# Joining the lower halves of seven-product pairs, two kinds of split buffers, three temporaries

## The chip, the cores and the metric

The kernel runs on one core of a Trainium2 chip. The metric is the device time of one execution in microseconds, as the median over several runs. Beside it there is one profiled execution, from which all rows of views are taken.

## The reference, cut to what matters

```python
D_MODEL, SEQ, D_FF = 2048, 256, 8192            # batch 1, 2 layers

def sq_relu_mlp(h, w1, w2):
    return jnp.square(jax.nn.relu(h @ w1)) @ w2

def reference(x, ...):
    for layer in range(2):
        h = rms_norm(x, norm_mixer_g[layer])
        if layer == 0:
            x = x + conv_module(h, ...)          # 2048x4096, depthwise 31, layer norm, 2048x2048
        else:
            x = x + mla(h, ...)                  # latent attention, 16 heads
        h = rms_norm(x, norm_mlp_g[layer])
        x = x + sq_relu_mlp(h, mlp_w1[layer], mlp_w2[layer])
    return rms_norm(x, final_norm_g)
```

Everything is float32. There are four stages: convolution, MLP 0, attention, MLP 1. The two MLPs multiply 256 rows by a 2048x8192 and an 8192x2048 matrix each.

## The kernel before

**Split products.** TensorE (PE) works on a rounded format (`F32R`), so each float32 operand is held as an upper part (the rounded copy) and a lower part (what the rounding left). A product is three matmuls: upper with upper, lower with upper, upper with lower (`mm3`, L201 to L205). The activations' parts are the stationary operand and the weights' parts are the moving one, 512 columns at a time; in the first product of an MLP it is the other way round (L655, L656).

**Streaming the weights.** `load` (L153) brings a tile `raw` of 128 x 2048 float32 from memory by a DMA that SyncE issues; there are three such buffers. A tile is split in two halves of 1024 columns: ScalarE copies the upper part (`hi`, L170), then VectorE subtracts it from the raw values and writes the lower part (`lo`, L174). `hi` and `lo` each go through one ring of `WB` = 6 buffers of 128 x 1024 (4 KB in each partition) that lives in `wpool` and is used by every stage. In the convolution and the attention the order of this work is written out by hand; in the MLPs a planner of the tile framework orders each engine's instructions from the program's order and from when operands are ready. On the chip every engine runs its own list in that order.

**An MLP** treats the 8192 inner columns in two halves (`hf`). For each half there is an up phase and a down phase.

The up phase has 8 groups `g` of 4 units; a unit is one raw tile and 32 pairs of matmuls into four accumulators. After a group, L673 to L677 add the two parts of the sums, square the positive values and scale them with a row `r2_row`. Then the result is split, plainly (L686, L687) or by `mixed_inputs`.

The down phase makes two sweeps over the 2048 output columns, each over one pair of 512-column blocks (class `Sums`, eight accumulators, all banks of PSUM). Its inner 32 blocks of 128 rows are taken two at a time, 16 pairs in a sweep. Eight of these (seven in the last half of MLP 1; the table `MIXED`) are **seven-product pairs**: the 2x2 block product of rows t, columns c and inner blocks j is made with seven products in place of eight by the Strassen-Winograd scheme, that is 21 matmuls instead of 24. The other pairs are plain. For a seven-product pair the weights need seven pieces of 512 columns: three blocks as they are (b11, b21, b22) and four sums (t1 to t4). `mixed_weights` (L490 to L510) makes them from one raw tile: a split of b11 and b21 (1024 columns), a split of b22 (512), three subtractions in place in the raw tile (L505 with 1024 columns, L506 and L507 with 512), a split of t1 and t3, a split of t4 and t2. That is four upper and four lower parts and three subtractions. `mixed_inputs` (L512 to L529) does the like for the activations, once for each pair in the up phase.

**Ending a sweep.** The four accumulators `u` of the seven-product pairs take part in several outputs. When the last of these pairs is done, `join` (L582 to L593) copies the first sum u1 to a temporary on ScalarE, forms three more sums on VectorE in three more temporaries, and adds the four results to the residual `xs` by `put`: by an accumulating DMA that GpSimd (POOL) issues where `by_dma` is set (five of the eight sweeps), else by VectorE. `close` (L595 to L605) adds the four other accumulators, in those sweeps two of them through temporaries copied by ScalarE and the DMA. The temporaries are the tiles `v` of the up phase, four buffers.

The very last sweep goes through `product_A`, which holds the splits of its last three units, finishes the rows of t = 0 first and then those of t = 1 in two halves of columns, so that the final norm can begin early.

The functions that the change touches, with the line numbers of the profile:

Of the kernel before, what the change touches and what calls it, by code (L numbers as in the profile page):

```python
# [18 lines left out]
P = 128  # L19
D = 2048  # L20
KC = D // P
T = 2
# [57 lines left out]
def trunk_kernel(  # L80
# [31 lines left out]
    wpool = ctx.enter_context(tc.tile_pool(name="wpool", bufs=2))  # L112
    small = ctx.enter_context(tc.tile_pool(name="small", bufs=2))
    psum, psum_cx = {}, [ExitStack()]

    def repool(name, **banks):

# [22 lines left out]
    def nm(s):  # L140
        uid[0] += 1
        return f"{s}_{uid[0]}"
# [21 lines left out]
    def upper_half(raw, h):  # L164

        _, nj, cols = raw.shape
        js = slice(h * nj // 2, (h + 1) * nj // 2)
        hi = wpool.tile([P, nj // 2, cols], F32R, tag="hi", name=nm("hi"), bufs=WB)
        lo = wpool.tile([P, nj // 2, cols], F32R, tag="lo", name=nm("lo"), bufs=WB)
        nc.scalar.activation(hi, raw[:, js, :], AF.Copy)  # L170
        return hi, lo, raw[:, js, :]

# [317 lines left out]
    def mixed_weights(raw):  # L490

        def halves(src):
            hi = wpool.tile(list(src.shape), F32R, tag="hi", name=nm("hi"), bufs=WB)
            lo = wpool.tile(list(src.shape), F32R, tag="lo", name=nm("lo"), bufs=WB)
            nc.scalar.activation(hi, src, AF.Copy)  # L497
            nc.vector.tensor_tensor(lo, src, hi.bitcast(F32), op=ALU.subtract)  # L498
            return [(hi[:, i, :], lo[:, i, :]) for i in range(src.shape[1])]
# [5 lines left out]
        nc.vector.tensor_tensor(top, raw[:, :, NB:], top, op=ALU.subtract)  # L505
        nc.vector.tensor_tensor(low[:, 1, :], low[:, 1, :], top[:, 0, :], op=ALU.subtract)  # L506
        nc.vector.tensor_tensor(low[:, 0, :], low[:, 0, :], low[:, 1, :], op=ALU.subtract)  # L507
        t1, t3 = halves(top)
        t4, t2 = halves(low)
        return b11, b21, b22, t1, t2, t3, t4  # L510

    def mixed_inputs(v, fh, fl):  # L512

        def halves(src, at, n):
            hi, lo = fh[:, at : at + n, :], fl[:, at : at + n, :]
            nc.scalar.activation(hi, src, AF.Copy)
            nc.vector.tensor_tensor(lo, src, hi.bitcast(F32), op=ALU.subtract)

        a = v.rearrange("p k (t n) -> p (k t) n", t=T)
# [4 lines left out]
        nc.vector.tensor_tensor(a21, a11, a21, op=ALU.subtract)  # L526
        nc.vector.tensor_tensor(a11, a22, a11, op=ALU.subtract)
        nc.vector.tensor_tensor(a12, a12, a11, op=ALU.subtract)
        halves(a, 3, 4)  # L529

    class Sums:
# [14 lines left out]
        def mixed(self, w, k, fh, fl, end):  # L546

            b11, b21, b22, t1, t2, t3, t4 = mixed_weights(load([rows(w, k, 2, self.n * NB, 2 * NB)], 2))
            u1, u6, u7, u5 = self.u
            work = [  # L550
                (u1, 0, b11), (u5, 6, t1), (u7, 4, t3), (u6, 3, t2),
                (self.e[0][0], 1, b21), (self.e[0][1], 5, b22), (self.e[1][0], 2, t4),
            ]
# [28 lines left out]
        def join(self, room):  # L582

            u1, u6, u7, u5 = self.u
            a, b, c, d = (room() for _ in range(4))
            nc.scalar.activation(a, u1, AF.Copy)
            self.put(0, 0, a if self.by_dma else u1)
            nc.vector.tensor_tensor(b, u6, a, op=ALU.add)
            nc.vector.tensor_tensor(c, u7, b, op=ALU.add)
            nc.vector.tensor_tensor(d, u5, c, op=ALU.add)  # L590
# [18 lines left out]
    def mlp(layer, ssq, next_gain, finish=None, before=None, beside=None, after_up=None):  # L609

        with ExitStack() as cx:
            mp = cx.enter_context(tc.tile_pool(name=f"mp{layer}", bufs=1, reuse_waits="tile"))
            nkh = FF // P // HALVES
            ng = nkh // 4
            nssq = None
            r2_row = mp.tile([P, S], F32, name=nm("r2_row"))
            repool(f"mlp{layer}", acc=8)

            def v_tile():
                return mp.tile([P, 2, S], F32, tag="v", name=nm("v"), bufs=4)  # L620

            def room():
                return v_tile().rearrange("p a n -> p (a n)")
# [10 lines left out]
            for hf in range(HALVES):  # L634
# [4 lines left out]
                gs = {}  # L639
                for g in range(ng):  # L640
                    ps = [acc_tile() for _ in range(4)]
                    if layer > 0 and hf == g == 0:
# [20 lines left out]
                    if g in mixed or g in plain[len(plain) + len(mixed) - N_MIXED :]:  # L663
                        shape = [P, 2, 7, P] if g in mixed else [P, 4, S]
                        gs[g] = [mp.tile(shape, F32R, tag=f"s{c}", name=nm(f"s{c}"), bufs=N_MIXED) for c in "hl"]
                    else:
                        gs[g] = [mp.tile([P, 4, S], F32R, tag=f"g{c}", name=nm(f"g{c}"), bufs=ng - N_MIXED) for c in "hl"]
                    gh, gl = gs[g]
                    for b2 in range(2):
                        v = v_tile()  # L670
                        for b in range(2):
                            o = ps[2 * b2 + b]
                            nc.scalar.activation(v[:, b, :], o[:, S:], AF.Copy)  # L673
                            nc.vector.tensor_tensor(v[:, b, :], o[:, :S], v[:, b, :], op=ALU.add)
                        nc.vector.scalar_tensor_tensor(out=v, in0=v, scalar=0.0, in1=v, op0=ALU.max, op1=ALU.mult)
                        row = r2_row.rearrange("p (a n) -> p a n", a=1).broadcast_to([P, 2, S])
                        nc.vector.tensor_tensor(v, v, row, op=ALU.mult)  # L677
                        if 2 * g + b2 in ms:
                            mixed_inputs(v, gh[:, b2], gl[:, b2])
                            continue  # L680
                        if g in mixed:
                            v = v.rearrange("p k (t n) -> p (k t) n", t=T)
                            h, l = gh[:, b2, : 2 * T, :], gl[:, b2, : 2 * T, :]
                        else:
                            h, l = (a[:, 2 * b2 : 2 * b2 + 2, :] for a in (gh, gl))
# [4 lines left out]

                def at_kt(i):
                    def at(k, t):
                        a = gs[k // 4][i]
                        if k // 4 in mixed:
                            return a[:, k % 4 // 2, k % 2 * T + t, :]
                        return a[:, k % 4, t * P : (t + 1) * P]
                    return at

                hi, lo = at_kt(0), at_kt(1)
# [1 line left out]
                due, rest = [], []  # L701

                def mixed_quad(sums, i):
                    g, b = divmod(ms[i], 2)
                    sums.mixed(w, k_lo + 4 * g + 2 * b, gs[g][0][:, b], gs[g][1][:, b], i == len(ms) - 1)

                split_end = last and finish is not None
                for n in range(0, NNB - 2 * split_end, 2):
# [599 lines left out]

    def rotary_tables(pool):

        place = pool.tile([P, 2, S], F32, tag="v", name=nm("v"), bufs=4).rearrange("p a n -> p (a n)")
        at = [0]

        def room(n):
# [629 lines left out]
```

## Time and profile before

| | |
|---|---|
| median of 3 runs | 1934.01 us (1933.93 to 1934.53) |
| profiled execution | 1934.31 us, its span 1932.5 us |
| TensorE matmuls (PE) | 1921.0 us busy, 10725 instructions |
| TensorE weight loads (PEld) | 1681.5 us |
| VectorE (DVE) | 1592.2 us, 2457 instructions |
| ScalarE (ACT) | 1095.6 us, 1636 instructions |
| GpSimd (POOL) | 249.0 us |
| DMA | 375.5 MB, mean 194 GB/s |

The profile is of one execution. Its span reaches from the first to the last instruction; the 1.8 us between the span and the execution's time lie around it. Busy times of the engines overlap. PE and PEld are the same engine's matmuls and loads of the stationary operand. A group or timeline row names the line of the kernel, the engine, the operation, what it writes and reads, the shapes and a count; "idle before" and the arrow tell how long the engine stood still and what it waited for. Line numbers can be a helper's: L170 and L174 are all plain splits, L203 to L205 all `mm3` products, L497 and L498 the splits of seven-product pairs.

### The profile page before, as it was taken

Reading aid. Unit: us, or ns where it says so; the run is one execution under the profiler, and the core shown is the slowest. Engines: PE = TensorE matmul, PEld = TensorE weight load, DVE = VectorE, ACT = ScalarE, POOL = GpSimd, SP = SyncE. Lnnn points to the kernel's source line nnn. Section 1 sums busy time; section 2 is a strip of 40 time slices with the busy share of each in tenths; the row PEclk is TensorE's granted clock in tenths of the full one; section 3 lists DMA queues with packets and bytes.
Section 4 is the critical chain, followed back from the end, with each engine's and each line's share of the span. In section 5 each row is a group of like instructions: output and inputs, shape, how many; then the busy total and the mean of one; then the engine's idle time right before and its main releaser. Section 6 shows DMA issues by size and latency. Waiting matters only on the chain.

```text
span 1932.5 us, 28477 instructions
## 1 busy us (share of the span) xinstructions
PE 1921.0 (99%) x10725; PEld 1681.5 (87%) x10725; DVE 1592.2 (82%) x2457; ACT 1095.6 (57%) x1636; POOL 249.0 (13%) x208
## 2 busy tenths in 40 slices
PE   9999999999999999999999999999999999999998
PEld 8999888888888888888898998888888888888887
DVE  7999988877999776799976766877789987678998
ACT  5667755554555545555576655555555554455554
POOL 6999200000010100000001420000000010000000
PEclk9999999999999999999999999999999999999999
DMA  7766456665585866655656545465646776665774
GB/s 230 214 183 189 153 189 206 193 194 177 175 251 194 263 195 187 194 174 196 217 176 175 142 134 192 155 216 186 188 162 225 222 248 212 191 196 175 231 219 150
DMA packets 230427, 375.50 MB, mean 194 GB/s; under 512 B 16392, under 2 KB 107792, under 8 KB 230032
## 3 DMA queue, kind: packets, MB, share of 16 engines
q1 hardware_dynamic: 224640, 363.28, 58.7%
q0 software_dynamic: 4320, 7.87, 2.2%
q10 hardware_dynamic: 1328, 2.52, 0.4%
q8 instruction: 84, 1.38, 0.3%
q14 instruction: 55, 0.45, 0.1%
HBM read 363.68 MB, written 2.10 MB: 189 GB/s over the span
## 4 chain that ended last, share of the span: by engine, by line
PE 97%; DVE 2%; DMA 0%; ACT 0%; issue 0%; ACTq 0%; DVEq 0%
PE acc L655 24%; PE acc L205 15%; PE acc L203 15%; PE acc L204 15%; PE acc L656 13%; PE acc L823 8%; PE acc L1287 2%; DVE sum L910 1%; DMA xs<-in_x 0%; PE acc L1535 0%; PE acc L1566 0%; PE acc L1565 0%; PE acc L1536 0%; PE acc L1564 0%; PE acc L1537 0%; PE tr L267 0%
## 5 line engine op out<-in xcount | busy, mean ns | idle before, releaser
L174 DVE TENSOR_TENSOR lo<-raw,hi 128x1024 fp32r<-128x1024 f32 (+2 forms) x509 | 602.2, 1197 | 232.3 <-ACT hi L170 226.6
L170 ACT ACTIVATE hi<-raw 128x1024 fp32r<-128x1024 f32 (+2 forms) x574 | 583.9, 1036 | 361.1 <-PE acc L655 203.7
L655 PE MATMUL acc<-xt,hi 128*128 128x512 f32 x2048 | 710.6, 390 | 0.0
L656 PE MATMUL acc<-xt,lo 128*128 128x256 f32 x2048 | 577.5, 282 | 0.0
L655 PEld LDWEIGHTS acc<-xt,hi 128*128 128x128 f32 x2048 | 384.3, 188 | 80.7
L656 PEld LDWEIGHTS acc<-xt,lo 128*128 128x128 f32 x2048 | 387.1, 189 | 0.2
L497 ACT ACTIVATE hi<-raw 128x1024 fp32r<-128x1024 f32 x248 | 228.7, 948 | 228.3 <-DVE raw L505 134.0
L498 DVE TENSOR_TENSOR lo<-raw,hi 128x1024 fp32r<-128x1024 f32 x248 | 263.9, 1087 | 27.6 <-ACT hi L497 22.5
L203 PE MATMUL acc<-hi,sh 128*128 128x512 f32 x514 | 200.1, 389 | 0.0
L205 PE MATMUL acc<-lo,sh 128*128 128x512 f32 x514 | 200.1, 389 | 0.0
L203 PE MATMUL acc<-hi,gh 128*128 128x512 f32 (+1 forms) x516 | 200.0, 388 | 0.0
L205 PE MATMUL acc<-lo,gh 128*128 128x512 f32 (+1 forms) x516 | 199.9, 387 | 0.0
L204 PE MATMUL acc<-hi,gl 128*128 128x512 f32 (+1 forms) x516 | 199.9, 387 | 0.0
L823 PE MATMUL acc<-xt,hi 128*128 128x256 f32 x1024 | 180.2, 281 | 0.3 <-ACT b L1106 0.2
L204 PE MATMUL acc<-hi,sl 128*128 128x512 f32 x450 | 175.1, 389 | 0.0
L578 POOL DMA_DIRECT2D xs<-v x30 | 26.5, 994 | 1136.4 <-DVE lo L174 703.2
L910 DVE SCALAR_TENSOR_TENSOR sum<-ub,w_dw,sum 128x256 f32<-128x256 f32 x409 | 164.3, 481 | 3.6 <-ACT sum L880 3.0
L174 POOL TENSOR_TENSOR lo<-raw,hi 128x1024 fp32r<-128x1024 f32 x65 | 155.0, 2410 | 17.3 <-ACT hi L170 17.3
L823 PEld LDWEIGHTS acc<-xt,hi 128*128 128x128 f32 x1024 | 154.8, 188 | 1.1 <-ACT xt L1090 0.6
L823 PE MATMUL acc<-xt,lo 128*128 128x256 f32 x512 | 139.2, 279 | 0.0
L205 PEld LDWEIGHTS acc<-lo,sh 128*128 128x128 f32 x514 | 96.5, 188 | 20.4 <-DVE lo L498 0.3
L204 PEld LDWEIGHTS acc<-hi,gl 128*128 128x128 f32 x516 | 96.9, 188 | 19.9
(314 smaller groups left out, 2531.3 us busy)
## 6 DMA issues: line engine op xcount, KB each, us to landing
raw<-in_mlp_w SPq DMA_DIRECT2D x255, 1024.0 KB, 5.5
raw<-in_conv_w_pw SPq DMA_DIRECT2D x62, 512.0 KB, 5.1
raw<-in_conv_w_pw SPq DMA_DIRECT2D x16, 1024.0 KB, 5.1
raw<-in_mla_w_o SPq DMA_DIRECT2D x16, 1024.0 KB, 5.7
raw<-in_mla_w_kv_up SPq DMA_DIRECT2D x32, 256.0 KB, 3.9
xs<-v POOLq DMA_DIRECT2D x30, 256.0 KB, 7.8
raw<-in_mla_w_in SPq DMA_DIRECT2D x8, 576.0 KB, 3.8
raw<-in_mla_w_in SPq DMA_DIRECT2D x4, 1024.0 KB
```

Of the source, the lines that this page charges most:

```text
L170: nc.scalar.activation(hi, raw[:, js, :], AF.Copy)
L174: eng.tensor_tensor(lo, raw, hi.bitcast(F32), op=ALU.subtract)
L203: nc.tensor.matmul(ps, sh, mh, start=start, stop=False)
L204: nc.tensor.matmul(ps, sl, mh, start=False, stop=False)
L205: nc.tensor.matmul(ps, sh, ml, start=False, stop=stop)
L497: nc.scalar.activation(hi, src, AF.Copy)
L498: nc.vector.tensor_tensor(lo, src, hi.bitcast(F32), op=ALU.subtract)
L655: nc.tensor.matmul(ps[b], wh[:, bs], xhl(k), start=k == 0, stop=False)
L656: nc.tensor.matmul(ps[b][:, :S], wl[:, bs], xh(k), start=False, stop=k == KC - 1)
L823: nc.tensor.matmul(pss[c][b][:, :S], w[i][:, bs], (xh, xl)[j](k), start=k == i + j == 0, stop=end and k == k0 + nk - 1 and (i, j) == terms ...
L910: nc.vector.scalar_tensor_tensor(out=out, in0=ubs[c][:, w : w + S], scalar=tap(c, w), in1=base, op0=ALU.mult, op1=ALU.add)
L1287: nc.tensor.matmul(ps2[b][t], x_kt(k, t), w[:, bs], start=k == g == i == 0, stop=k == KC - 1 and i == len(group) - 1,)
```

## The change

- **Joined halves.** `mixed_weights` looks at the raw tile as four pieces and splits three of them, b21, b22 and b11, as one tile of 1536 columns. The first subtraction takes 1024 columns with one operand that repeats one piece and another that reads two pieces backwards. Two subtractions of 512 columns and two splits of 1024 follow. `mixed_inputs` splits three of the four untouched pieces at once. The numbers of the products in `Sums.mixed` follow the new places.
- **Two kinds of split buffers.** The buffers are no longer one ring in `wpool`: each stage opens a pool of its own (`open_halves`), at the same place in memory. The convolution and the attention have six and six as before. In the MLPs there are two of kind "a" (for the first half of a plain tile and for the 1536 columns, 6 KB in each partition) and three of kind "b" (for the second half and for the 1024-column splits of a seven-product pair), of upper and lower parts each.
- **Three temporaries.** `join` uses one temporary again, and the `v` tiles have three buffers. u1 is always added to the residual by VectorE.
- The tiles for the split activations are arranged by pairs instead of groups, and `r2_row` lies in an existing scratch tile. `MIXED` is the same.

```diff
-N_MIXED = 4
+SPLIT_BUFS = {"a": 2, "b": 3}
...
+    def open_halves(cx, name, kinds=False):
+        halves_of[:] = [cx.enter_context(tc.tile_pool(name=name, bufs=1, reuse_waits="tile"))]
+        two_kinds[0] = kinds
+
+    def in_halves(shape, kind=None):
+        kind = kind if two_kinds[0] else None
+        n = WB if kind is None else SPLIT_BUFS[kind]
+        return [halves_of[0].tile(shape, F32R, tag=c + (kind or ""), name=nm(c), bufs=n) for c in ("hi", "lo")]
...
-        hi = wpool.tile([P, nj // 2, cols], F32R, tag="hi", name=nm("hi"), bufs=WB)
-        lo = wpool.tile([P, nj // 2, cols], F32R, tag="lo", name=nm("lo"), bufs=WB)
+        hi, lo = in_halves([P, nj // 2, cols], "ab"[h])
         nc.scalar.activation(hi, raw[:, js, :], AF.Copy)
...
-        b11, b21 = halves(raw[:, :, :NB])
-        (b22,) = halves(raw[:, 1:2, NB:])
-        top = raw[:, 0, :].rearrange("p (c n) -> p c n", c=2)
-        low = raw[:, 1, :].rearrange("p (c n) -> p c n", c=2)
-        nc.vector.tensor_tensor(top, raw[:, :, NB:], top, op=ALU.subtract)
-        nc.vector.tensor_tensor(low[:, 1, :], low[:, 1, :], top[:, 0, :], op=ALU.subtract)
-        nc.vector.tensor_tensor(low[:, 0, :], low[:, 0, :], low[:, 1, :], op=ALU.subtract)
-        t1, t3 = halves(top)
-        t4, t2 = halves(low)
+        r = raw.rearrange("p j (c n) -> p (j c) n", c=2)
+        h1, l1 = in_halves([P, 3, NB], "a")
+        nc.scalar.activation(h1, r[:, :3, :], AF.Copy)
+        nc.vector.tensor_tensor(l1, r[:, :3, :], h1.bitcast(F32), op=ALU.subtract)
+        nc.vector.tensor_tensor(
+            r[:, 2:4, :], r[:, 3:4, :].broadcast_to([P, 2, NB]), r[:, 2:0:-1, :], op=ALU.subtract
+        )
+        nc.vector.tensor_tensor(r[:, 1, :], r[:, 1, :], r[:, 2, :], op=ALU.subtract)
+        nc.vector.tensor_tensor(r[:, 0, :], r[:, 0, :], r[:, 1, :], op=ALU.subtract)
+        b21, b22, b11 = ((h1[:, i, :], l1[:, i, :]) for i in range(3))
+        t = []
+        for i in (2, 0):
+            h2, l2 = in_halves([P, 2, NB], "b")
+            nc.scalar.activation(h2, r[:, i : i + 2, :], AF.Copy)
+            nc.vector.tensor_tensor(l2, r[:, i : i + 2, :], h2.bitcast(F32), op=ALU.subtract)
+            t += [(h2[:, j, :], l2[:, j, :]) for j in range(2)]
+        t1, t3, t4, t2 = t
...
-        a11, a21, a12, a22 = (a[:, i, :] for i in range(4))
-        halves(a[:, 0:1, :], 0, 1)
-        halves(a[:, 2:4, :], 1, 2)
+        a12, a22, a11, a21 = (a[:, i, :] for i in range(4))
+        halves(a[:, 0:3, :], 0, 3)
...
-            a, b, c, d = (room() for _ in range(4))
+            a, c, d = (room() for _ in range(3))
             nc.scalar.activation(a, u1, AF.Copy)
-            self.put(0, 0, a if self.by_dma else u1)
-            nc.vector.tensor_tensor(b, u6, a, op=ALU.add)
-            nc.vector.tensor_tensor(c, u7, b, op=ALU.add)
+            x = self.place(0, 0)
+            nc.vector.tensor_tensor(x, u1, x, op=ALU.add)
+            nc.vector.tensor_tensor(a, u6, a, op=ALU.add)
+            nc.vector.tensor_tensor(c, u7, a, op=ALU.add)
             nc.vector.tensor_tensor(d, u5, c, op=ALU.add)
-            nc.vector.tensor_tensor(b, u5, b, op=ALU.add)
-            for (t, n), o in (((1, 0), c), ((1, 1), d), ((0, 1), b)):
+            nc.vector.tensor_tensor(a, u5, a, op=ALU.add)
+            for (t, n), o in (((1, 0), c), ((1, 1), d), ((0, 1), a)):
                 self.put(t, n, o)
...
+            open_halves(cx, f"halves{layer}", kinds=True)
...
-            r2_row = mp.tile([P, S], F32, name=nm("r2_row"))
+            r2_row = scratch[:, :S]
...
-                return mp.tile([P, 2, S], F32, tag="v", name=nm("v"), bufs=4)
+                return mp.tile([P, 2, S], F32, tag="v", name=nm("v"), bufs=3)
...
+        open_halves(cx, "halvesc")
...
+        open_halves(cx, "halvesa")
```

More of the change, by code (lines that the diff above doesn't have):

```diff
@@ L550, in mixed @@
             work = [
-                (u1, 0, b11), (u5, 6, t1), (u7, 4, t3), (u6, 3, t2),
-                (self.e[0][0], 1, b21), (self.e[0][1], 5, b22), (self.e[1][0], 2, t4),
+                (u1, 2, b11), (u5, 4, t1), (u7, 6, t3), (u6, 5, t2),
+                (self.e[0][0], 0, b21), (self.e[0][1], 3, b22), (self.e[1][0], 1, t4),
             ]
@@ L662, in mlp @@
                         beside = None
-                    if g in mixed or g in plain[len(plain) + len(mixed) - N_MIXED :]:
-                        shape = [P, 2, 7, P] if g in mixed else [P, 4, S]
-                        gs[g] = [mp.tile(shape, F32R, tag=f"s{c}", name=nm(f"s{c}"), bufs=N_MIXED) for c in "hl"]
-                    else:
-                        gs[g] = [mp.tile([P, 4, S], F32R, tag=f"g{c}", name=nm(f"g{c}"), bufs=ng - N_MIXED) for c in "hl"]
-                    gh, gl = gs[g]
+                    both = [2 * g, 2 * g + 1]
+                    if g % 2 == 0:
+                        tiles = [mp.tile([P, 2, 7, P], F32R, tag=f"s{c}", name=nm(f"s{c}"), bufs=ng // 2) for c in "hl"]
+                        for b2, p in enumerate(both):
+                            fs[p] = [a[:, b2] for a in tiles]
+                    elif g == 1:
+                        fs[2] = [mp.tile([P, 7, P], F32R, tag=f"o{c}", name=nm(f"o{c}")) for c in "hl"]
+                        fs[3] = [mp.tile([P, 2 * T, P], F32R, tag=f"p{c}", name=nm(f"p{c}")) for c in "hl"]
+                    else:
+                        tiles = [mp.tile([P, 2, 2 * T, P], F32R, tag=f"g{c}", name=nm(f"g{c}"), bufs=ng // 2 - 1) for c in "hl"]
+                        for b2, p in enumerate(both):
+                            fs[p] = [a[:, b2] for a in tiles]
                     for b2 in range(2):
@@ L703, in mixed_quad @@
                 def mixed_quad(sums, i):
[L704 to L705 removed]
+                    sums.mixed(w, k_lo + 2 * ms[i], *fs[ms[i]], i == len(ms) - 1)
                 split_end = last and finish is not None
@@ L1309, in rotary_tables @@
     def rotary_tables(pool):
-        place = pool.tile([P, 2, S], F32, tag="v", name=nm("v"), bufs=4).rearrange("p a n -> p (a n)")
+        place = pool.tile([P, 2, S], F32, tag="v", name=nm("v"), bufs=3).rearrange("p a n -> p (a n)")
         at = [0]
```

26 lines of the change are left out of this document (8 added, 18 removed).

## The prediction, on record before the change was run

> **What bounds the kernel now.** I read the page first: busy time by engine, then the chain that ended last.
>
> ```profile
> span 1932.5 us, 28477 instructions
> ...
> PE 1921.0 (99%) x10725; PEld 1681.5 (87%) x10725; DVE 1592.2 (82%) x2457; ACT 1095.6 (57%) x1636; POOL 249.0 (13%) x208
> ...
> PE 97%; DVE 2%; DMA 0%; ACT 0%; issue 0%; ACTq 0%; DVEq 0%
> ```
>
> TensorE is busy for 99% of the span and carries 97% of the chain. VectorE at 82% and ScalarE at 57% are behind it. Then the windows by stage (columns: length, then busy us and count of PE, PEld, DVE, ACT, POOL, then clock and DMA).
>
> ```profile
> 300.00:478.00 178.00, 178.00 (x1029) 157.75 (x1028) 139.41 (x242) 95.47 (x140) 0.00 (x0) 1.00 0.60 190
> 478.00:560.00 82.00, 82.00 (x364) 67.91 (x363) 77.30 (x86) 45.79 (x53) 3.65 (x4) 1.00 0.60 196
> 641.00:819.00 178.00, 178.00 (x1027) 157.73 (x1027) 126.15 (x187) 90.77 (x128) 1.77 (x2) 1.00 0.66 205
> 1842.00:1924.50 82.50, 82.50 (x377) 68.78 (x375) 76.58 (x97) 46.55 (x65) 1.75 (x2) 1.00 0.58 183
> 1924.50:1932.50 8.00, 0.23 (x2) 0.03 (x1) 3.18 (x12) 1.42 (x3) 0.00 (x0) 0.77 0.37 131
> ```
>
> In the MLPs PE has no gap: an up phase (the first product, 1024 matmuls) takes 178.0 us and a sweep of the down phase (the second product, one pair of 512-column blocks) about 82. Two up phases agree at 178.0 although VectorE is busy for 139 us in one and 126 us in the other: its load does not set their pace. VectorE fills 94% of a sweep, so there it is close behind. The change leaves PE's matmuls as they are, so it can win only where PE waits now, and that is little. It can lose wherever it makes a split arrive late.
>
> **What is saved.** These are the groups, shapes apart (count, then busy us, mean ns).
>
> ```profile
> L498 DVE TENSOR_TENSOR lo<-raw,hi 128x1024 fp32r<-128x1024 f32 x186 | 225.5, 1221 | 27.6 <-ACT hi L497 22.5 <-PE acc L205 0.6
> L497 ACT ACTIVATE hi<-raw 128x1024 fp32r<-128x1024 f32 x186 | 195.0, 1058 | 222.3 <-DVE raw L505 134.0 <-DVE raw L507 34.5 <-PE acc L204 23.6
> L505 DVE TENSOR_TENSOR raw<-raw 128x1024 f32<-128x1024 f32 x62 | 75.5, 1218 | 0.2
> L507 DVE TENSOR_TENSOR raw<-raw 128x512 f32<-128x512 f32 x62 | 42.8, 691 | 1.7
> L498 DVE TENSOR_TENSOR lo<-raw,hi 128x512 fp32r<-128x512 f32 x62 | 42.4, 684 | 0.0
> L497 ACT ACTIVATE hi<-raw 128x512 fp32r<-128x512 f32 x62 | 38.4, 619 | 6.0 <-PE acc L204 5.9
> ```
>
> A seven-product pair now costs VectorE four 1024-column and three 512-column operations, ScalarE three and one. Joined, one 1024 and one 512 become one 1536. Columns beyond 512 cost 1221 − 684 = 537 ns per 512, so a 1536 takes about 1.76 us. Against 1.22 + 0.68 that saves 0.15 us of latency per pair. Operations overlap, though: in the timeline below two 1024 splits span 2.35 us, so they start 1.13 to 1.14 us apart, less than the 1.22 that one lasts. By start to start the saving is about 0.07 us. Over 62 pairs it is 4 us (by latency 9) of VectorE time, and about as much of ScalarE's; 31 pairs of inputs lose one small operation on each engine too. All of it lies beside PE, so it is worth 0.
>
> The Trainium skill ("Perfetto Trace Analysis", section "Optimizing Scalar/DVE Operations") gives about 60 ns of overhead per VectorE instruction, half of what is seen as latency: by it the saving is an estimate of 62 × 0.06 = 3.7 us, and the trace's 0.07 and 0.15 agree. The same section says that where these engines are not saturated but cause bubbles on others, "breaking up instructions may allow work to be completed sooner", which speaks against joining here; that is the late first product weighed next.
>
> **The joined tile comes whole.** Its first product (b11) waits for 1536 columns instead of 1024: 0.54 us later on ScalarE, and later again on VectorE. This matters where two seven-product pairs follow each other.
>
> ```profile
> 838.97 1.82 DVE L498 TENSOR_TENSOR lo<-raw,hi 128x1024 fp32r<-128x1024 f32 x2
> 840.71 1.22 DVE L505 TENSOR_TENSOR raw<-raw 128x1024 f32<-128x1024 f32 x1
> 836.70 2.35 DVE L174 TENSOR_TENSOR lo<-raw,hi 128x1024 fp32r<-128x1024 f32 x2
> 847.47 1.22 DVE L505 TENSOR_TENSOR raw<-raw 128x1024 f32<-128x1024 f32 x1
> 850.06 2.52 DVE L498 TENSOR_TENSOR lo<-raw,hi 128x1024 fp32r<-128x1024 f32 x2
> 851.43 0.39 PE L203 MATMUL acc<-hi,sh 128*128 128x512 f32 x1
> ```
>
> Pair after pair VectorE needs 847.47 − 840.71 = 6.76 us; a plain pair needs 838.97 − 836.70 = 2.27. PE starts a matmul every 0.2267 us (1841.91 to 1842.14 in a row below is one), so a seven-product pair gives it 21 × 0.2267 = 4.76 us of work and a plain one 24 × 0.2267 = 5.44. VectorE loses 2.0 us of lead per seven-product pair and gains 3.2 per plain one. Here the lower part of the fifth product's weights is ready at 850.06 + 1.2 = 851.3, 0.15 us ahead of its first matmul. It is wanted only in the third matmul, 0.45 later, so 0.6 us is left. The wait of a joined copy (0.4 us) eats most of that. For the three sweeps that begin with two such pairs I take 0.1 each, 0.3 together (0 to 3).
>
> **The rings.** Before, one ring of six hi and six lo buffers runs through the whole program, and a split goes ahead six half units. Now it is two "a" and three "b" in the MLP, laid out anew in the same memory at each stage. Inside an up phase "a" and "b" alternate every half unit of 178.0 / 64 = 2.78 us. With two "a" tiles a unit's first half can be filled only once the first half of the unit two before it is used up: 2 × 5.56 − 2.78 − (1.06 + 1.22 + a little for the two hand-overs) leaves a lead of some 5.9 us. That is enough and costs 0.
>
> **Borders of the stages.** Old and new tiles of a border share memory. Before, only the next free slot of the ring counted. I laid the tiles out by size and order: hi at 0 to 24 KB and lo at 24 to 48 KB with six each; in the MLP a-hi, a-lo, b-hi, b-lo at 0, 12, 24 and 36 KB. From convolution to MLP the first "a" tile falls on one free in time: 0. From MLP 0 to attention the first lower part falls on the last "b" tile, which PE reads until the MLP ends at 984.04.
>
> ```profile
> 976.11 0.75 DVE L174 TENSOR_TENSOR lo<-raw,hi 128x576 fp32r<-128x576 f32 x1
> 984.66 1.27 DVE L601 TENSOR_TENSOR xs<-acc,xs 128x512 f32<-128x512 f32 x2
> 984.04 0.29 PE L203 MATMUL acc<-hi,xt 128*128 128x288 f32 x1
> ```
>
> That split now ends at 976.9; then it can start only at about 984.4, lasts 0.75, and is wanted 0.3 us after 984.04: a stall of 0.9 us if VectorE takes it first, 2.1 if it adds the two sums first (L601). Queued behind it are the next splits and the last sums. I take 1.5 (0 to 2.6). From attention to MLP 1 the first "a" lower tile falls on the attention's last split.
>
> ```profile
> 1239.67 1.23 DVE L174 TENSOR_TENSOR lo<-raw,hi 128x1024 fp32r<-128x1024 f32 x1 [1.49 <-ACT hi L170]
> 1240.84 1.37 DVE L388 TENSOR_TENSOR xs<-acc,xs 128x512 f32<-128x512 f32 x2
> 1241.32 0.40 PE L655 MATMUL acc<-xt,hi 128*128 128x512 f32 x1
> ```
>
> The split that is now begun at 1239.67 waits until 1241.3 + 0.4 and, behind the two sums, begins at about 1242.2 and ends at 1243.4; it is wanted by the second matmul at 1241.55: 1.9 us (0 to 2.4).
>
> **The last sweep**, from 1842, has the least lead of all. Before, its first seven-product pair is copied early, into the free ring.
>
> ```profile
> 1836.14 1.58 ACT L497 ACTIVATE hi<-raw 128x1024 fp32r<-128x1024 f32 x2 [3.16 <-DMA raw<-in_mlp_w]
> 1842.48 0.59 ACT L604 ACTIVATE v<-acc 128x512 f32<-128x512 f32 x1
> ...
> 1841.91 0.39 PE L205 MATMUL acc<-lo,gh 128*128 128x512 f32 x1
> 1842.14 0.39 PE L203 MATMUL acc<-hi,gh 128*128 128x512 f32 x1
> ...
> 1890.73 2.52 DVE L498 TENSOR_TENSOR lo<-raw,hi 128x1024 fp32r<-128x1024 f32 x2
> 1891.78 0.39 PE L203 MATMUL acc<-hi,sh 128*128 128x512 f32 x1
> ```
>
> With two "a" tiles, both still read by the sweep before until about 1841.5, that copy moves from 1836.14 to 1841.5, and with it VectorE's seven operations, 1 to 4 us later than now since it can do other splits meanwhile. At 1891.78 no lead is left today (the lower part ends at 1890.73 + 1.2 = 1891.9, wanted at 1892.2), and a plain pair with a seven-product pair gives back only 3.2 − 2.0 = 1.2 us each time. I take a stall of 2.5 us in sum, from 0 (lead regained by then) to 5.
>
> **Three temporaries, sums, tail.**
>
> ```profile
> xs<-v POOLq DMA_DIRECT2D x30, 256.0 KB, 7.8
> 1836.03 0.86 POOL L578 DMA_DIRECT2D xs<-v  x1 [6.68 <-DVE v L589]
> 1839.47 1.78 POOL L578 DMA_DIRECT2D xs<-v  x2 [2.58 <-DVE v L590]
> ```
>
> Five sweeps add by DMA; of their 30 DMAs five become VectorE additions (5 × 0.69 = 3.4 us, beside PE). But the first temporary, whose DMA was issued early, is now free only after the last of three: two left at 1839.47, and ScalarE's copy into a temporary at 1842.48 would wait until a landing up to 7.8 us after issue, with the next upper parts queued behind it. First products into those banks come a plain pair (5.4 us) later, so I take 0.5 for all (0 to 5). In the tail the last block holds three units' splits until the end, with two "a" tiles for them: 0.4 (0 to 3), on top of the 8 us of 1924.50 to 1932.50.
>
> **Sum:** 0 + 0.3 + 0 + 1.5 + 1.9 + 2.5 + 0.5 + 0.4 = 7.1 us on the profiled execution of 1934.31, which is 0.3 above the median of 1934.01. On the median: 1941.1.
>
> **The rivals.**
> 1. *Nothing is late.* The tiles do not collide as I laid them out, or other work is put in front, and the lead carries the last sweep: 1934 to 1937.5, say 1935.5. For it: PE's only visible wait inside the MLPs now is nearly nil, and leads of 6 us remain. Against: the last sweep's lead of zero.
> 2. *The joined subtraction with one half repeated and one read backwards runs at half pace.* A pair would need 6.76 + 1.2 us and a pair with a plain one 10.2, all that PE has (4.76 + 5.44): no lead is regained, each of seven sweeps would lose about 2 to 3 us more, 1955. No row has a reversed operand; one that is repeated is read at the normal pace:
>
> ```profile
> 391.68 0.69 DVE L677 TENSOR_TENSOR v<-v,r_row 128x512 f32<-128x512 f32 x1
> ```
>
> 3. *The tail or the temporaries decide:* ScalarE blocked 5 us in each of two sweeps, or the last block put in another order: 1948 to 1955.
> 4. *Faster:* the up phases' pace is set by a waiting hi/lo split. 512 pairs at 0.2267 + 0.1133 would take 174.1 us instead of 178.0; all four at that pace would give 1934.0 − 15.6 = 1918.4. It decides from about 1 us per phase on. Against: the same 178.0 us at unequal loads.
>
> **How the numbers follow.** This kernel can be told from no change beyond about 0.2%, 3.9 us: below 1930.1 or above 1937.9. Chances: forecast (1937.9 to 1948) 0.58; rival 1 0.30; rival 2 0.03; rival 3 0.06; rival 4 0.03. Slower is 0.58 + 0.03 + 0.06 = 0.67, same 0.30, faster 0.03. The range 1934.6 to 1948 leaves out rivals 2 to 4 and the lower fifth of rival 1, under 0.2. The forecast's own range is 1937.9 to 1948.
>
> **What would show it.** Right: PE waits of 1 to 3 us at the two borders (near 984 and 1242) and waits on a lower part from about 1850 to 1925; up phases at 178.0; L498-type work in three upper and three lower splits, VectorE down by 4 to 9 us. Wrong: no PE wait at the borders (then the tiles do not collide), waits in the up phases (two "a" are too few), or a 1024-column difference far over 1.22 us.

## The result, and the profile after

The changed kernel takes 1984.31 us (median of 4, 1982.92 to 1985.37) against 1933.98 before: a ratio of 1.0259 (95% interval 1.0241 to 1.0277), 50.3 us slower. The prediction was 1941.1 with a range up to 1948.0: the direction is right, the size is far off.

The page of the changed kernel:

```profile
span 1982.4 us, 28046 instructions
...
PE 1946.5 (98%) x10725; PEld 1678.6 (85%) x10725; DVE 1591.7 (80%) x2369; ACT 1084.9 (55%) x1543; POOL 244.7 (12%) x203
...
issue 13%; DMA 2%; DVE 2%; PE 1%; ACT 1%; POOL 0%; DVEq 0%; ACTq 0%; POOLq 0%
```

PE still looks 98% busy. But its busy time grew by 25 us with the same 10725 matmuls, so about half of the loss does not show as idle time. Matmuls start 0.23 us apart and are recorded with 0.39 us each, so a delay shorter than the difference leaves no gap between two records, and a longer one shows only in part. The chain of waits, 97% PE before, has fallen apart and says little. A count of busy shares would have missed the loss here; the waits of PE name it (line waited for: us, times, longest):

```profile
PE acc L216 <- DVE lo L519: 10.6, 16, 1.0
PE acc L214 <- ACT hi L518: 6.7, 12, 1.0
PE acc L669 <- DVE lo L185: 2.4, 2, 1.4
PE acc L214 <- ACT hi L181: 2.0, 1, 2.0
PE acc L216 <- DVE lo L185: 2.0, 1, 2.0
```

L518 and L519 are the splits of t1 t3 and of t4 t2, the last two of each seven-product pair; L507 and L508 are the joined 1536-column split; L181 and L185 the plain ones; L214 to L216 the matmuls of `mm3`. So PE waits for the pair's last splits, some 0.6 us at a time, and not for the joined one, which comes first.

Where the time went, from the first matmul of each stage to the first of the next in the two traces:

| stage | before, us | after, us | difference |
|---|---|---|---|
| convolution | 300.3 | 300.2 | −0.1 |
| MLP 0: up, sweep, sweep | 177.7, 81.6, 81.6 | 179.8, 86.3, 88.0 | +2.0, +4.7, +6.4 |
| MLP 0, second half | 177.5, 81.6, 83.7 | 177.7, 85.5, 87.7 | +0.2, +3.9, +4.1 |
| attention | 257.3 | 261.1 | +3.8 |
| MLP 1: up, sweep, sweep | 177.8, 81.6, 81.6 | 179.8, 85.2, 87.8 | +2.0, +3.6, +6.2 |
| MLP 1, second half, with the tail | 177.5, 82.3, 90.4 | 177.5, 83.4, 102.4 | 0.0, +1.1, +12.0 |

The eight sweeps lose 42.0 us, the three borders 7.8. Two windows show a sweep: the second of MLP 0 before, and the same after (length, then busy us and count of PE, PEld, DVE, ACT and POOL, then TensorE's granted clock, the DMA share and GB/s).

```profile
560.00:641.26 81.26, 81.26 (x360) 67.27 (x359) 75.16 (x79) 46.91 (x51) 5.26 (x6) 1.00 0.70 223
```

```profile
567.00:654.30 87.30, 84.42 (x359) 67.30 (x357) 76.56 (x72) 46.37 (x44) 4.40 (x5) 0.98 0.66 208
```

VectorE does no more work (76.6 us busy against 75.2), but the sweep lasts 6 us longer: it stands idle at the wrong moments. (The clock of 0.98 is a stretch of 3.4 us at half clock behind two waits, some 1.6 us of the 6; the last section has it.) The timeline of the changed kernel shows which. First VectorE, then ScalarE, then one row of PE:

```profile
535.48 1.76 DVE L508 TENSOR_TENSOR lo<-raw,hi 128x1536 fp32r<-128x1536 f32 x1 [1.04 <-ACT hi L507]
537.15 1.22 DVE L519 TENSOR_TENSOR lo<-raw,hi 128x1024 fp32r<-128x1024 f32 x1
...
539.42 1.22 DVE L185 TENSOR_TENSOR lo<-raw,hi 128x1024 fp32r<-128x1024 f32 x1
540.56 0.69 DVE L512 TENSOR_TENSOR raw<-raw 128x512 f32<-128x512 f32 x1
...
533.95 1.49 ACT L507 ACTIVATE hi<-raw 128x1536 fp32r<-128x1536 f32 x1 [0.93 <-DMA raw<-in_mlp_w]
535.35 1.04 ACT L518 ACTIVATE hi<-raw 128x1024 fp32r<-128x1024 f32 x1
536.43 1.06 ACT L181 ACTIVATE hi<-raw 128x1024 fp32r<-128x1024 f32 x1
...
538.43 0.50 PE L216 MATMUL acc<-lo,sh 128*128 128x512 f32 x1 [0.76 <-DVE lo L519]
```

The joined copy that ScalarE begins at 533.95 belongs to the *next* pair. It stands ahead of this pair's last copy (535.35), and it waits 0.93 us for its own transfer. The last subtraction of this pair (L513) ends at 533.30, so for most of that wait ScalarE could have done the other copy. On VectorE the next pair's 1.76 us subtraction (535.48) then stands ahead of this pair's last lower part (537.15), for which PE waits 0.76 us at 538.43. At 539.42 a plain tile's split goes ahead of two subtractions of an earlier pair in the same way. ScalarE's list in the built program shows the same without times, at the first two seven-product pairs of a sweep (the number behind `raw` names the tile, in the order of the program; two copies of other lines are left out):

```
L507 hi <- raw_714  1536      L518 hi <- raw_721  1024
L518 hi <- raw_714  1024      L518 hi <- raw_721  1024
L507 hi <- raw_721  1536      L181 hi <- raw_728  1024
L518 hi <- raw_714  1024      ...
L181 hi <- raw_728  1024
```

(read down the left column, then the right). Over the program 62 upper copies stand ahead of an earlier raw tile's last copy; in the kernel before there are none. One ring hands out its slots in the program's order, so no tile could overtake another. Two rings let a tile of one kind take a free slot while an older tile waits for the other kind, or for its subtractions, and the planner then queues it first.

### The profile page after: what moved, and what is told of

Its sections match the earlier page's. It is cut to its first block, busy times and chain, and to the rows that moved or that the text cites. A ratio compares the mean times of both kernels' runs of the same rounds, so it can differ in the third digit from the quotient of the medians.

```text
span 1982.4 us, 28046 instructions
## 1 busy us (share of the span) xinstructions
PE 1946.5 (98%) x10725; PEld 1678.6 (85%) x10725; DVE 1591.7 (80%) x2369; ACT 1084.9 (55%) x1543; POOL 244.7 (12%) x203
## 5 line engine op out<-in xcount | busy, mean ns | idle before, releaser
L181 ACT ACTIVATE hi<-raw 128x1024 fp32r<-128x1024 f32 (+2 forms) x574 | 586.9, 1037 | 409.2 <-PE acc L668 287.2
L185 DVE TENSOR_TENSOR lo<-raw,hi 128x1024 fp32r<-128x1024 f32 (+2 forms) x509 | 605.4, 1196 | 228.8 <-ACT hi L181 224.8
L518 ACT ACTIVATE hi<-raw 128x1024 fp32r<-128x1024 f32 x124 | 130.9, 1055 | 203.8 <-DVE raw L509 145.5
L214 PE MATMUL acc<-hi,sh 128*128 128x512 f32 x514 | 203.7, 396 | 7.0 <-ACT hi L518 6.7
L216 PE MATMUL acc<-lo,sh 128*128 128x512 f32 x514 | 199.0, 401 | 11.2 <-DVE lo L519 10.6
L589 POOL DMA_DIRECT2D xs<-v x25 | 22.1, 1005 | 1170.2 <-DVE v L601 1117.9
L519 DVE TENSOR_TENSOR lo<-raw,hi 128x1024 fp32r<-128x1024 f32 x124 | 151.2, 1219 | 18.9 <-ACT hi L518 18.5
L185 POOL TENSOR_TENSOR lo<-raw,hi 128x1024 fp32r<-128x1024 f32 x65 | 155.2, 2413 | 17.3 <-ACT hi L181 17.3
L214 PE MATMUL acc<-hi,gh 128*128 128x512 f32 (+1 forms) x388 | 151.3, 390 | 2.0 <-ACT hi L181 2.0
L215 PE MATMUL acc<-hi,gl 128*128 128x512 f32 (+1 forms) x388 | 151.1, 389 | 0.0
L216 PE MATMUL acc<-lo,gh 128*128 128x512 f32 (+1 forms) x388 | 150.6, 390 | 0.1
L216 PEld LDWEIGHTS acc<-lo,sh 128*128 128x128 f32 x514 | 94.2, 188 | 46.8 <-DVE lo L519 28.3
L508 DVE TENSOR_TENSOR lo<-raw,hi 128x1536 fp32r<-128x1536 f32 x62 | 108.9, 1757 | 24.7 <-ACT hi L507 23.3
```

The source lines that it names most:

```text
L185: eng.tensor_tensor(lo, raw, hi.bitcast(F32), op=ALU.subtract)
L214: nc.tensor.matmul(ps, sh, mh, start=start, stop=False)
L215: nc.tensor.matmul(ps, sl, mh, start=False, stop=False)
L216: nc.tensor.matmul(ps, sh, ml, start=False, stop=stop)
L508: nc.vector.tensor_tensor(l1, r[:, :3, :], h1.bitcast(F32), op=ALU.subtract)
L518: nc.scalar.activation(h2, r[:, i : i + 2, :], AF.Copy)
```

## The experiments

The first set asked whether the loss comes from the order, the joined operation, the number of tiles or the temporaries. Losses are against the kernel before, from the traces, by the stages of the table above.

**One ring instead of two kinds** (`one_ring_6`, `one_ring_5`). The plain groups' activations share one tile to make room, so the work is kept but not the values of those groups.

```diff
+        if two_kinds[0]:
+            ts = [halves_of[0].tile([P, 3 * NB], F32R, tag=c, name=nm(c), bufs=WB) for c in ("hi", "lo")]
+            _, a, b = shape
+            return [t[:, : a * b].rearrange("p (a b) -> p a b", a=a) for t in ts]
```

> The changed kernel, but in the MLPs all splits (1024 and 1536 columns) share one ring of six upper and six lower tiles of 6 KB, handed out in program order. Room for it comes from the plain groups of split activations, which share one tile, so the second product uses wrong values there; the work is the same. In the changed kernel the eight sweeps together take 42 us more than before, the borders of the stages about 7.5. Theory ORDER (with two rings of tiles the planner can put the next pair's 1536-column split, or a plain split, ahead of this pair's last splits, which are needed first; 62 such places in ScalarE's list, none before, none here): the sweeps lose less than 8 us against before, total 1936 to 1950. Theory JOIN (the 1536-column operation itself is late and blocks): sweeps still lose 25 us or more, total over 1962. Theory TEMPORARIES (three instead of four): sweeps still lose 25 or more. Theory FEW TILES (five in place of six): as ORDER.

> As one_ring_6 with five upper and five lower tiles: the same number of tiles as the changed kernel's two and three, but in one ring and so in program order. ORDER: sweeps lose less than 15 us, total 1938 to 1957. FEW TILES: sweeps lose about what they lose in the changed kernel, total 1970 or more. JOIN and TEMPORARIES: over 1962.

Measured: 1993.59 and 1993.73 us. By their totals both are misses for ORDER and lie where the rivals had them (over 1962, 1970 or more), but through other stages: convolution +12.4 and +12.3 us, attention +14.7 and +16.3, up phases +20.5 and +17.7. PE's waits in `one_ring_6`:

```profile
PE acc L671 <- ACT hi L184: 24.6, 2, 12.3
PE acc L217 <- ACT gh L705: 14.9, 4, 3.7
```

The first is the wait for the first upper part of each MLP, 12.3 us; why it comes so late with these larger pools was not isolated. The second is no border at all: at the end of each of the four up phases PE waits 3.7 us for the shared activations (`gh`). The sweeps, which the expectation was about, lose 11.0 and 13.9 in place of 42.0, more than the 8 that ORDER gave `one_ring_6` and within its 15 for `one_ring_5`; at least three of the eight are within 0.3 us of before in each. Most of what they lose is not their own: four of the eight begin in a stretch of half clock behind these waits, or soon run into one (see the last section). By the lengths of those stretches an estimate of some 10 of the 11.0 and 8 of the 13.9 is half clock, and in `one_ring_5` 2.9 more is a wait for shared activations. So the joined operation and three temporaries cost the sweeps next to nothing where the tiles are handed out in order, and five tiles in order are far better than five in two kinds: the number of tiles alone is not the cause. But the shared tile disturbs the comparison, since the splits also run ahead while PE waits for it, and a cleaner one was wanted.

**More tiles of two kinds** (`kinds_3_4`): `SPLIT_BUFS = {"a": 3, "b": 4}`, room as above.

> The changed kernel with three 'a' and four 'b' tiles (seven instead of five), room from shared activation tiles as above. Its lists still have 71 places where a later split stands ahead of an earlier one. ORDER: sweeps still lose 25 us or more, total 1962 to 1990. FEW TILES: sweeps lose less than 12 us, total 1936 to 1955. JOIN and TEMPORARIES: over 1962.

Measured: 2010.73 us, above the ranges of ORDER and FEW TILES, again through the other stages; only "over 1962" for the joined operation and the temporaries holds it. The sweeps lose 27.4 us with seven tiles out of order, as ORDER has it and twice what they lose with five in order. Some 10 of the 27.4, by the same estimate, is half clock that four sweeps take over from the wait at the end of the up phase.

**The joined operation made two again** (`unjoined`), into the same tiles:

```diff
-        nc.scalar.activation(h1, r[:, :3, :], AF.Copy)
-        nc.vector.tensor_tensor(l1, r[:, :3, :], h1.bitcast(F32), op=ALU.subtract)
+        for i in (slice(0, 3, 2), slice(1, 2)):
+            nc.scalar.activation(h1[:, i, :], r[:, i, :], AF.Copy)
+            nc.vector.tensor_tensor(l1[:, i, :], r[:, i, :], h1[:, i, :].bitcast(F32), op=ALU.subtract)
```

> The changed kernel, but the 1536-column upper copy and lower subtraction are each made as one operation of 1024 columns (b11, b21) and one of 512 (b22) into the same tile. 62 places out of order as in the changed kernel. JOIN: sweeps lose less than 12 us, total 1940 to 1955. ORDER, FEW TILES, TEMPORARIES: total 1975 to 1992, since VectorE's work grows by 4 us and nothing else is changed.

Measured: 1963.06 us, 1.0148 (1.0133 to 1.0163); the sweeps lose 23.9. Between the two expectations: joining has a part, but more than half stays.

**The order alone** (`in_order`). Nothing else is touched:

```diff
+    def in_order(engine, ins):
+        if two_kinds[0]:
+            if engine in newest:
+                tc.add_manual_dep(
+                    ins.ins, newest[engine],
+                    mybir.DependencyInfo(mybir.DependencyClass.NoSync, mybir.DependencyReason.DATA), reason="in_order",
+                )
+            newest[engine] = ins.ins.name
...
-        nc.scalar.activation(hi, raw[:, js, :], AF.Copy)
+        in_order("scalar", nc.scalar.activation(hi, raw[:, js, :], AF.Copy))
```

and so for every split and subtraction of the weights; the class `NoSync` is an order of issue without a wait.

> The changed kernel with one thing added: in the MLPs every split operation is queued on its engine (ScalarE, VectorE) behind the split operation before it in the program, an order without a wait. Tiles, rings (two 'a', three 'b'), memory and operations are those of the changed kernel; nothing is left out and no tile is shared. ORDER: the sweeps lose 5 to 18 us in place of 42 (the eight sweeps of one_ring_5, five tiles in order, lost 14), the borders 8 as in the changed kernel: total 1945 to 1962. Theory BLOCKING (it is the tiles of two sizes themselves, whatever the order): no change, 1975 to 1992.

Measured: 1951.57 us, 1.0087 (1.0072 to 1.0102). The sweeps lose 10.4 in place of 42.0, with the same tiles, sizes and operations. ORDER is shown, BLOCKING falls. The same pair in this kernel, VectorE and then ScalarE (L521 and L520 are the joined split, L532 and L531 the others):

```profile
531.78 2.52 DVE L532 TENSOR_TENSOR lo<-raw,hi 128x1024 fp32r<-128x1024 f32 x2
534.45 1.76 DVE L521 TENSOR_TENSOR lo<-raw,hi 128x1536 fp32r<-128x1536 f32 x1 [0.15 <-ACT hi L520]
...
530.53 1.06 ACT L531 ACTIVATE hi<-raw 128x1024 fp32r<-128x1024 f32 x1 [3.29 <-DVE raw L522]
531.98 1.06 ACT L531 ACTIVATE hi<-raw 128x1024 fp32r<-128x1024 f32 x1 [0.39 <-DVE raw L526]
532.94 1.47 ACT L520 ACTIVATE hi<-raw 128x1536 fp32r<-128x1536 f32 x1
```

Both last splits are done before the next pair's joined one begins.

**In order and unjoined** (`in_order_unjoined`): both edits.

> in_order with the 1536-column operations made as 1024 and 512 again, into the same tiles. ORDER alone: within 4 us of in_order. If joining costs by itself even in order: 6 to 15 us faster than in_order.

Measured: 1946.53 us, 1.0062 (1.0047 to 1.0077), 5.0 us less than `in_order`; the sweeps lose 5.4. The forecast for ORDER alone (within 4) is missed by one, and the one for joining (6 to 15) too. The first sweep of three halves loses 0.7 instead of 1.8, the last 2.6 instead of 4.2. So joining by itself costs 5 us with these tiles when the lists are in order. Out of order it costs 18 to 21 us (42.0 against 23.9; 1984.3 against 1963.1). That fits an operation that is the dearer in front the longer it lasts, but this reason was not tested by itself.

**Four temporaries again** (`in_order_four`): `join` and four `v` buffers as before, in `in_order`; a smaller activation tile makes the room.

> in_order with the join of before: four temporaries, u1 added by DMA where the sweep adds by DMA. In the changed kernel ScalarE waited 15.6 us in five places for a DMA to free a temporary. If those waits reach PE: 3 to 10 us faster than in_order, mostly in the sweep after one that adds by DMA and in the last. If they are covered: within 2 us.

Measured: 1952.48 us, within 1 us of `in_order`. ScalarE does wait for a temporary, in the changed kernel and in `in_order`:

```profile
ACT v L616 <- DMA xs<-v: 15.6, 5, 5.1
```

```profile
ACT v L629 <- DMA xs<-v: 26.5, 6, 7.1
```

but in order these waits are covered: with four temporaries 1.9 us is left of the 26.5, and the time does not fall.

**The order on VectorE alone** (`order_vector_only`):

> The changed kernel with the order of splits fixed on VectorE alone; ScalarE's list keeps its 62 places where a later tile's upper copy stands ahead of an earlier tile's last. If ScalarE's order is what makes splits late: the sweeps still lose 20 us or more, total 1962 to 1995. If VectorE's order (the long lower splits that stand in front) does it: like in_order, 1948 to 1956.

Measured: 1980.87 us, sweeps +38.2. VectorE's order is worth little while ScalarE's list, which sets when a split can come, stays as it is. ScalarE's order without VectorE's was not run.

**Two rings in the kernel before** (`two_rings_before`): the ring of six becomes `tag="hi" + "ab"[h]` with three each; b11 b21 and t1 t3 are "a", b22 and t4 t2 are "b".

> The kernel before with its one ring of six (hi and lo) made two rings of three, same size of tiles, same memory, same operations: one ring for the first half of a plain tile and for the splits of b11 b21 and of t1 t3, one for the second half and for b22 and t4 t2. ScalarE's and VectorE's lists then have 33 places out of order where before has none. ORDER: 6 to 25 us slower than before, in the sweeps. If only the change's 1536-column tiles make it costly: within 4 us of before.

Measured: 1937.72 us, 1.0019 (1.0010 to 1.0029); borders and up phases unchanged, sweeps +4.2. The sign is as ORDER has it, the size is not (6 to 25 expected): at 3.7 us the run meets the other expectation, within 4. But that one named the 1536-column tiles alone as what makes a wrong order costly, and this does not hold either: with small operations and tiles of two kinds the order costs 18.5 us (23.9 in `unjoined` against 5.4 in `in_order_unjoined`), with the joined one 31.6 (42.0 against 10.4). Here there are six tiles and 33 places out of order in place of 62; which of the two makes it cheap was not separated.

**The borders** (`pools_by_stage`, `in_order_two_pools`, `in_order_unj_pools`). In the first the kernel before opens its ring anew in each stage (`halves_of[0].tile(...)` for `wpool.tile(...)`).

> The kernel before with one thing changed: its ring of six is opened anew in each stage instead of once. If the collisions at the borders come from opening anew: the first up phase of each MLP and the attention lose what they lose in the changed kernel, 2.0 + 3.8 + 2.0, total 1938 to 1943. If they come from the two sizes: total 1934 to 1936. The sweeps must not change.

Measured: 1946.22 us, 1.0060 (1.0045 to 1.0075), more than the 1938 to 1943 expected: first up phases +4.0 and +4.3, attention +2.2, the sweeps unchanged within 0.1. Opening anew costs by itself, whatever the sizes. The changed kernel at the first border (ScalarE, VectorE, PE):

```profile
289.51 1.05 ACT L181 ACTIVATE hi<-raw 128x1024 fp32r<-128x1024 f32 x1
300.54 0.63 ACT L424 ACTIVATE scratch<-xs 128x512 f32<-128x512 f32 x1 [9.98 <-DVE xs L399]
...
299.75 1.37 DVE L399 TENSOR_TENSOR xs<-acc,xs 128x512 f32<-128x512 f32 x2 [7.92 <-PE acc L216]
301.16 0.43 DVE L345 STREAM_TRANSPOSE ca<-xs 32x256 f32<-32x256 f32 x1
301.53 1.17 DVE L185 TENSOR_TENSOR lo<-raw,hi 128x1024 fp32r<-128x1024 f32 x1
...
302.75 0.74 PE L669 MATMUL acc<-xt,lo 128*128 128x256 f32 x4 [1.42 <-DVE lo L185]
```

ScalarE stands still for 10 us and VectorE for 8 before the stage ends, where before they split ahead (copies at 292.12, 294.84 and 297.56). The copy at 289.51 is the MLP's first and is done at 290.56; its lower part is made only at 301.53, behind the stage's last sums (L399), when PE already wants it. At attention and MLP 1 it is alike:

```profile
1006.84 3.47 DVE L185 TENSOR_TENSOR lo<-raw,hi 128x576 fp32r<-128x576 f32 x5
1007.65 0.40 PE L216 MATMUL acc<-lo,xt 128*128 128x288 f32 x1 [1.97 <-DVE lo L185]
```

```profile
1265.86 1.37 DVE L399 TENSOR_TENSOR xs<-acc,xs 128x512 f32<-128x512 f32 x2 [7.92 <-PE acc L216]
1267.64 1.17 DVE L185 TENSOR_TENSOR lo<-raw,hi 128x1024 fp32r<-128x1024 f32 x1
```

> in_order with the upper parts in one pool and the lower parts in another, each opened per stage, so that tiles of old and new stages meet elsewhere in memory (upper over upper, lower over lower). If the place of the tiles sets the loss at the borders: the sum of first up phases and attention (plus 1.8 + 3.8 + 1.7 in in_order) moves by over 2 us, down where a new tile falls on one freed early; sweeps as in in_order, +10. If opening a pool costs by itself: the same 7.3.

> in_order_two_pools and unjoined together: sweeps as in in_order_unjoined (+5 us against before), borders as in in_order_two_pools. Total 1936 to 1947; it beats the kernel before in no theory, since PE has no wait there that any of this removes.

Measured: 1951.63 and 1947.09 us, the second just above its range. Upper and lower parts in pools of their own leave the two MLP borders at 1.7 and 1.6 us; the attention's falls from 3.8 to 2.2, as it also does in `unjoined`, `in_order_unjoined`, `in_order_four` and `pools_by_stage`. The traces show why: PE's wait at that border is the same 1.97 us (1.83 in `pools_by_stage`), but in the changed kernel and in `in_order` a stretch of half clock follows it, and in these runs none does. So 2.2 us is the border's own loss and 1.6 is clock, and the sum of the three borders fell from 7.3 to 5.6 nearly all through the clock. The place of a tile, as far as this run moves it, is thus not what sets the loss. Whether the lower part waits for room or only for its turn behind the last sums is left open. No variant beats the kernel before.

## Why the prediction was wrong, point by point

**Right:** PE has nothing to gain, and VectorE's saving is worth nothing. The joined subtraction takes 1757 ns, against 1.76 us worked out; the subtraction with a repeated and a reversed operand 1222 ns, against 1218 before, so rival 2 falls:

```profile
L508 DVE TENSOR_TENSOR lo<-raw,hi 128x1536 fp32r<-128x1536 f32 x62 | 108.9, 1757 | 24.7 <-ACT hi L507 23.3 <-PE acc L215 1.1
L519 DVE TENSOR_TENSOR lo<-raw,hi 128x1024 fp32r<-128x1024 f32 x124 | 151.2, 1219 | 18.9 <-ACT hi L518 18.5
L509 DVE TENSOR_TENSOR raw<-raw 128x1024 f32<-128x1024 f32 x62 | 75.8, 1222 | 1.3
```

Of its splits VectorE is rid of 7.8 us (225.5 + 42.4 before, 108.9 + 151.2 now), within the 4 to 9 forecast; yet its total only goes from 1592.2 to 1591.7. Up phases lose nothing outside the borders, so two "a" tiles are enough there. Rival 4, a faster up phase, falls: 177.5 and 177.7 us.

**The step that failed** is the term for the sweeps, 0.3 us for three of them and 0 for the rest. It took the engines' lists of the kernel before, with the new durations put in. That a second ring also frees the *order* was not thought of: the prediction treated the rings as a number of slots and worked out only leads. Its rival 1 even named "other work is put in front", but as something that would save time. The first seven sweeps lost 30.0 us, and `in_order` takes 23.8 of these back. With the lists in order they lose 6.2, with the joined operation undone as well 2.8. That is the size the prediction was arguing about, and still above its 0.3. (A small misreading there: the product at 851.43 is the pair's fourth, not its fifth; the 0.15 and 0.6 us of lead stand.)

**The last sweep and tail**, 2.5 + 0.4, measured 12.0; in order 4.2. The mechanism (less lead, nothing left at a late pair of two) fits the ordered kernel: two of its waits there, 0.31 and 0.71 us, stand at the very matmul that the prediction named at 1891.78 and just behind it. The rest goes with the order; in the changed kernel it holds a wait of 2.0 us for a plain upper part (the row PE acc L214 <- ACT hi L181) and 1.6 us of half clock behind it.

**The temporaries**, 0.5: within noise of 0 by `in_order_four`, with ScalarE's waits covered. As forecast.

**The borders**, 0 + 1.5 + 1.9 = 3.4, measured 2.0 + 3.8 + 2.0 = 7.8. The one from attention to MLP 1 is right in size. The one before the attention is 2.2 by its wait, within the 0 to 2.6 given, and 1.6 by the half clock behind it, which the prediction did not have. The one after the convolution was put at nothing, from slots laid out by hand, and is the same wait as the others. That slots decide was not shown; `in_order_two_pools` speaks against it at the MLP borders.

**The Trainium skill's** sentence that the prediction weighed ("Perfetto Trace Analysis", section "Optimizing Scalar/DVE Operations"), on breaking up instructions where an engine that is not saturated causes bubbles on others, agrees with the runs: breaking the joined operation up again gained 5.0 us in order and 21.2 out of order.

Of the 50 us by the traces, the order accounts for 32 (42.0 − 10.4), joining for 5 more once the lists are in order, and the borders for 8; the remaining 5 in the sweeps, half of it in the last, go with the new tiles and were not split further. About 5 of the 50 is half clock that followed waits: 3.3 in the sweeps, where the ordered kernel has none, and 1.6 at the attention.

## What to carry to other kernels

A ring of buffers that is shared by all tiles does two things: it limits how far ahead work may run, and it keeps that work in order. Whoever splits it by kind should look at the engines' lists afterwards, or fix the order where a later tile may overtake an earlier one that is needed first; here that edit alone was worth 33 us. And a pool that is opened anew at each stage takes the look-ahead across the border with it, some 2 to 4 us each time.

## What the runs showed of the hardware

**A wait costs PE more than its idle time shows.** In the changed kernel the matmul at 576.27 starts 1.44 us after the one before it, 1.21 more than the usual 0.23, while the row gives 1.05 us of idle time. It is recorded with 0.50 us instead of 0.39, and the next starts 0.34 us later instead of 0.23. So this wait costs 1.05 + 0.16 + 0.11 us; over the 30 waits of more than 0.15 us in the eight sweeps the step behind the waiting matmul is 0.11 us longer on average.

```profile
574.83 0.40 PE L215 MATMUL acc<-hi,sl 128*128 128x512 f32 x1
576.27 0.50 PE L216 MATMUL acc<-lo,sh 128*128 128x512 f32 x1 [1.05 <-DVE lo L519]
576.61 0.39 PE L214 MATMUL acc<-hi,sh 128*128 128x512 f32 x1
576.84 0.40 PE L215 MATMUL acc<-hi,sl 128*128 128x512 f32 x1
```

**Some waits are followed by a stretch at half clock.** Here are the attention's border in the changed kernel, with the stretch, and the same border in `in_order_unjoined`, without one, each with its window (the clock is the third number from the end):

```profile
1008.59:1012.00 3.41, 3.41 (x17) 3.39 (x17) 2.29 (x7) 1.43 (x4) 0.00 (x0) 0.50 0.75 209
1008.28 0.29 PE L214 MATMUL acc<-hi,xt 128*128 128x288 f32 x1
1008.41 0.30 PE L215 MATMUL acc<-hi,xt 128*128 128x288 f32 x1
1008.99 0.44 PE L215 MATMUL acc<-hi,xt 128*128 128x288 f32 x1
1009.23 0.44 PE L216 MATMUL acc<-lo,xt 128*128 128x288 f32 x1
```

```profile
989.63 0.40 PE L229 MATMUL acc<-lo,xt 128*128 128x288 f32 x1 [1.97 <-DVE lo L196]
989.63:1000.00 10.37, 10.37 (x81) 10.37 (x82) 7.33 (x15) 6.40 (x16) 0.00 (x0) 1.00 0.63 185
```

The matmuls start 0.24 us apart instead of 0.13, and the stretch of 3.41 us costs about 1.6 us: the attention loses 3.8 us with it and 2.2 without. In the changed kernel such stretches begin at 578.50, 1008.59 and 1957.49, 0.9 to 2.2 us after the end of a wait of 1.0 to 2.0 us; the kernel before has none while PE is at work. The wait of 1.97 us is the same in both traces above, so such a wait makes a stretch possible but does not always bring one; what decides it was not isolated.
